# One low-part operation per weight piece, and background steps moved from the second attention to the first FFN

## The chip, the cores and the metric

The kernel runs on 1 core of one Trainium2 chip. The metric is device time in microseconds (us) of one launch. Three timed runs of the kernel before took 968.81, 970.23 and 971.09 us; the median is 970.23.

## The reference, cut

A block of 256 tokens of width 1024 passes through three layers: attention and a SwiGLU FFN twice, then a conformer convolution module and an FFN with a short convolution. Everything is fp32. Each layer has six modulation vectors, which come from one vector `c` and a 1024 x 6144 matrix; they scale, shift and gate what the layer does.

```python
c_act = silu(c)
for i in range(2):
    mod = c_act @ ada_w[i] + ada_b[i]                       # six vectors of 1024
    sh_a, sc_a, g_a, sh_f, sc_f, g_f = split(mod, 6)
    h = rms_norm(x, norm_g[i, 0]) * (1 + sc_a) + sh_a
    y = moba_attention(h, ...) if i == 0 else diff_attention(h, ...)
    x = x + g_a * rms_norm(y, norm_g[i, 1])
    h = rms_norm(x, norm_g[i, 2]) * (1 + sc_f) + sh_f
    g, u = split(h @ ffn_w_in[i], 2)                        # 1024 x 5632
    x = x + g_f * rms_norm((silu(g) * u) @ ffn_w_out[i], norm_g[i, 3])
# third layer: the same frame with its own c and matrix, a conformer module and conv_ffn
```

## The kernel before, in words

**Stages.** Six stages follow one another: first attention, first FFN, second attention (the one with two softmaxes a head), second FFN, conformer, last FFN. Between two of them stand a residual sum, a norm and transposes (`residual`, `norm_T`). In this profile the first attention runs to about 150 us, the first FFN to 338, the second attention to 473, the second FFN to 660, the conformer to 775.

**Weights.** Each weight is read once. `load` takes a raw buffer (a pool of four, 1 MiB each; a few parked tiles at the start) and issues the DMA on SP's queue. `split` then makes of each half of a raw buffer, a piece of 128 x 1024, a high part (ScalarE, line 108, a copy rounded to fp32r) and a low part (VectorE, line 110, raw minus high). Before the change the low part is two operations of 512 columns: one for each half of a row piece, or, for pieces of column blocks, one for each four of the eight row tiles. High and low parts live in `hlp`, which has eight buffers for each, so four units can be split ahead of TensorE, and the four raw buffers stand behind them. `mm3` (lines 135 to 137) makes three matmuls of each product: high x high, high x low, low x high. `cols_unit` loads 1024 rows of 256 columns, `rows_unit` 256 rows of 1024 columns, `half_unit` four row tiles of two spans.

**An FFN's loop** (`swiglu`). Eleven chunks of 256 hidden columns. Chunks 0 and 1 go first with tokens in rows. Then pass d = 0 to 10 computes the hidden columns of chunk d + 2 (`up_cols`, two column units, 96 matmuls of 256 columns; pass 7 does two chunks, the later ones none), and multiplies chunk d with `w_out` (`down_half`, one row unit, 24 matmuls of 512 columns). After `up_cols` and after the row unit of a pass `bg_step` is called: 17 calls in passes 0 to 7, two in each of 0 to 6, three in 7. The second FFN has hooks in its passes that build the conformer's stationary operands (`conv_weights`, line 463), the first has small loads and transposes (`columns`, `conv_taps`).

**An attention** projects v (four row units), then q and k of two heads at a time (eight column units). The heads' softmax chains run beside the matmuls (`block`): scores on TensorE, `sc` and `mn` on VectorE (618), exp on ScalarE (620), a transpose on TensorE (635), the product with v (641), and in the second attention a norm of each head: POOL (650, 652), `on` on VectorE (654), a transpose (657), `ol` on VectorE (659). At the end comes the output projection (four row units). `bg_step` is called after each of the 16 units of an attention.

**Background vectors.** The first two modulation vectors are made at the start. The other 16 are made by the generator `background`, one after the other, four steps a vector. A step loads 1 MiB of the matrix (`mod_load`, SP's queue, a raw buffer) and adds it to `gemv` in two VectorE operations of 1024 columns (lines 202 and 204), which are ordered behind the newest low part. The last step sums over the partitions with 8 small matmuls (232), adds the bias (235), multiplies by a gain (211 or 213), and stores the row to `scratch` with a DMA on SP's queue (214). The loads of the next bias and gain into the single tiles `bquad` and `gquad` (line 180) are on SP's queue too. `fetch`, at the end of a stage, reads the vectors that it needs and runs the steps that are missing.

**The plans.** `bg_plan(steps, slots, skip)` spreads so many steps over so many calls of `bg_step`, after `skip` calls: each call takes the steps left over the slots left, rounded up. So (16, 17) gives one step a call, and (20, 17) two in each of the first three calls and one afterwards. The line is `plans = ((12, 10, 2), (16, 17), (12, 12), (20, 17), (0, 0), (4, 4, 4))`, one entry a stage; the steps sum to 64.

**Order.** Tile's scheduler orders each engine's queue and SP's from the program order and its own model. Each queue then runs in that order.

Of the kernel before, what the change touches and what calls it, by code (L numbers as in the profile page):

```python
# [36 lines left out]
def bucket_rows():  # L37
    """One-hot rows [32, 384]: column m is the bucket of rel = 255 - m (columns past 255 are masked)."""
    exact = N_BUCKETS // 2
    rel = np.maximum(255 - np.arange(384), 0)  # L40
    nf = np.maximum(rel, 1).astype(np.float32)
    large = exact + (np.log(nf / np.float32(exact)) / np.float32(math.log(MAX_DISTANCE / exact))
                     * np.float32(N_BUCKETS - exact)).astype(np.int32)
    large = np.minimum(large, N_BUCKETS - 1)
    b = np.where(rel < exact, rel, large)
    return (b[None, :] == np.arange(N_BUCKETS)[:, None]).astype(np.float32)
# [3 lines left out]
def net(ctx: ExitStack, tc: tile.TileContext, a, out):  # L50
# [17 lines left out]

    # ---------------------------------------------------------------- weights

# [12 lines left out]
    def parked(*tags):  # L83
        """Room for the two pieces of a unit in tiles that rest between two parts of the network."""
        rooms = []
        for tag in tags:
            if tag == "q":
                for _ in range(2):
                    t = two.tile([P, 1024], F32R, name="park", tag=tag)
                    rooms.append(t)  # L90
            else:
                t = big.tile([P, 2, 1024], F32R, name="park", tag=tag)
                rooms += [t[:, 0, :], t[:, 1, :]]
        return rooms

    def split(raw, blocks=False, rooms=None):
        pieces = []
        for j in range(2):
            r = raw[:, 1024 * j:1024 * j + 1024]
            if rooms:  # L100
                h, l = rooms[2 * j], rooms[2 * j + 1]
            else:
                h = hlp.tile([P, 1024], F32R, name="h")
                l = hlp.tile([P, 1024], F32R, name="l")
            if blocks:
                r = raw.rearrange("p (k n) -> p k n", k=8)[:, :, j * P:j * P + P]
                h, l = (t.rearrange("p (k n) -> p k n", k=8) for t in (h, l))
            newest["high"] = nc.scalar.activation(h, r, AF.Copy).ins  # L108
            for k in (slice(0, 4), slice(4, 8)) if blocks else (slice(0, 512), slice(512, 1024)):
                newest["split"] = nc.vector.tensor_sub(l[:, k], r[:, k], h[:, k].bitcast(F32)).ins  # L110
            pieces.append((h, l))
        return pieces

    def rows_unit(w, k0, c0, rooms=None):
        """Two row tiles of 1024 columns; a piece is one row tile."""
        return split(load(lambda raw: [(
            raw.rearrange("p (k n) -> p k n", k=2),
            w[k0 * P:k0 * P + 256, c0:c0 + 1024].rearrange("(k p) n -> p k n", p=P))]), rooms=rooms)

    def cols_unit(w, c):  # L120
        """All eight row tiles of 256 columns; a piece is one block of 128 columns."""
        return split(load(lambda raw: [(raw.rearrange("p (k n) -> p k n", k=8),
                                        w[:, c:c + 256].rearrange("(k p) n -> p k n", p=P))]), blocks=True)

    def half_unit(w, q, cols, rooms=None):
        """Four row tiles of two 256 column spans; a piece is two row tiles of 512 columns."""
        def parts(raw):
            v = raw.rearrange("p (k n) -> p k n", k=4)
            return [(v[:, :, i * 256:i * 256 + 256],
                     w[512 * q:512 * q + 512, c:c + 256].rearrange("(k p) n -> p k n", p=P))  # L130
                    for i, c in enumerate(cols)]
        return [tuple(t.rearrange("p (k n) -> p k n", k=2) for t in hl) for hl in split(load(parts), rooms=rooms)]
# [5 lines left out]

    # -------------------------------------------------------------- constants

# [17 lines left out]

    # ------------------------------------------------------------- modulation

# [17 lines left out]
    def load_quad(vec, t, queue=nc.sync):  # L178
        """A row of 1024 as four spans of 256, on partitions 0, 32, 64 and 96."""
        queue.dma_start(t.rearrange("(g r) n -> g r n", r=32)[:, 0, :], vec.rearrange("(g n) -> g n", g=4))  # L180
        return t

    def mod_load(w, j, r, halved=False):
        """Rows 8 p + 2 r and 8 p + 2 r + 1 of a vector's 1024 columns."""
        src = w[:, j * D:j * D + D].rearrange("(p k) n -> p k n", k=8)[:, 2 * r:2 * r + 2, :]
# [4 lines left out]
    def mod_sum(w, j, c):  # L190
        """Per-partition partial sums of c @ w[:, vector j]; yields after each quarter, the tile last."""
        t = None
# [24 lines left out]
    def quads(ps, c, k, src, start, stop):  # L217
        """ps[32 q:32 q + 32] += c[k] * the span q of 256 of the row, summed over the partitions."""
        for q in range(4):
# [4 lines left out]
    def mod_vector(w, b, j, g, slot, c):  # L224
        """Vector j of a layer's modulation, into the scratch; yields after each quarter of the rows."""
        bq = load_quad(b[j * D:j * D + D], bquad)
# [12 lines left out]

    # vector j of a layer: shift, scale, gate of the mixer, then of the ffn  # L240
    jobs = []
# [42 lines left out]
    def first_norm(T):  # L284
        """The first layer's scale and shift, turned into columns, and what they make of x: only the shift's part
        waits for all of their weights."""
        bias = [bquad, gquad]
# [56 lines left out]

    # ------------------------------------------------------------ small inputs

    nb = big.tile([P, NH, S], F32, name="nb")

    def bias_tiles():
        """nb[p, h, k] = -bias of head h for query - key = 127 + p - k, masked where negative: the rows of the  # L350
        Toeplitz matrix start one further left on each partition, which is a step back, so they are read
        upside down and flipped by the permutation."""
        st = hlp.tile([P, 1024], F32, name="stage", tag="h")
# [77 lines left out]
    def conv_taps():  # L431
        """taps[32 j + c, m, 4 t + g] = tap 4 m + j of channel 128 t + 32 g + c."""
        w = a["a_dw_w_2"][0]
# [16 lines left out]
    def conv_weights(ts):  # L450
        """Stationary operands of the depthwise convolution: four taps of 32 channels stacked on the rows."""
        for t in ts:
# [15 lines left out]

    # ------------------------------------------------------------------ norms

# [4 lines left out]
    def rstd_of(ss):  # L475
        """(the sum of the two columns + eps)^-0.5."""
        v = small.tile([P, 1], F32, name="var")
# [5 lines left out]
    def scaled(src, by, tag="hn"):  # L483
        """The two halves of a row times a vector, and what normalises the row."""
        ss = small.tile([P, 2], F32, name="ss")
# [44 lines left out]
    def project(T, w, c0, tags=(), between=None, early=0, before=None):  # L530
        """[256 tokens, 1024] = T @ w[:, c0:c0+1024]; yields the two banks of each half of the tokens."""
        ps = [[acc.tile([P, 512], F32, name="acc") for _ in range(2)] for _ in range(2)]
# [19 lines left out]
    def cols_matmul(ps, T, unit, between=None):  # L552
        """ps[:, b, :] = features of block b, all 256 tokens."""
        for b, (wh, wl) in enumerate(unit):
# [5 lines left out]
    def lead(T, w, cols, count):  # L560
        """As cols_matmul for the first 2 * count blocks of both column spans, with tokens in rows until turned;
        the first half of the tokens is done before the second is asked for."""
        units, tiles = [], []
# [36 lines left out]

    # -------------------------------------------------------------- attention

    def block(diff, h, blk, q, kk, v, T):
        """One head, 128 queries: their attention over the keys up to them, into T[:, h, block]."""
        nk = P * (blk + 1)
# [109 lines left out]

    # -------------------------------------------------------------------- ffn

# [85 lines left out]

    # -------------------------------------------------------------- conformer

# [172 lines left out]

    # ---------------------------------------------------------------- network

# [13 lines left out]
    stages.append((2, 5, lambda T: conv_ffn(T, a["f_up_w_2"][0], a["f_down_w_2"][0])))  # L994
    plans = ((12, 10, 2), (16, 17), (12, 12), (20, 17), (0, 0), (4, 4, 4))

# [41 lines left out]
```

## Time and profile before

| | |
|---|---|
| timed runs | 968.81, 970.23, 971.09 us |
| span of the profiled execution | 967.0 us |
| TensorE busy | 928.9 us (96%) |
| VectorE busy | 767.5 us (79%) |
| ScalarE busy | 495.1 us (51%) |
| low parts, line 110, 512 columns, `l` and parked tiles | 548 and 24 operations of 0.68 us |
| background, lines 202 and 204 | 16 and 112 operations |
| DMA | 244 MB, mean 252 GB/s |

The span goes from the first to the last instruction of the profiled execution, whose own device time isn't given apart from the three runs; their median is 3.2 us longer than this span. Matmuls are pipelined, so a busy TensorE isn't one at its peak: its rows of busy time hide short waits, and starts of matmuls show them. A line number is that of the kernel; the changed kernel's lines after 109 are one less.

### The profile page before, as it was taken

How to read it: one execution, taken by the hardware profiler on the slowest of the kernel's cores; microseconds unless marked ns; L12 is line 12 of the kernel's file. 1: busy time of each engine (PE TensorE's matmuls, PEld its weight loads, DVE VectorE, ACT ScalarE, POOL GpSimd, SP SyncE). 2: the span in 40 equal slices, each digit the busy share in tenths (PEclk: the TensorE clock that was granted, in tenths of full speed). 3: DMA queues.
4: the chain of work that ended last, by engine and by line, in shares of the span. 5: the costliest groups of instructions: out<-in, count | busy, mean ns of one | idle time of the engine just before them, and what ended most of it. 6: DMA issues, size and time to landing. Idle time of an engine off the chain costs nothing.

```text
span 967.0 us, 17220 instructions
## 1 busy us (share of the span) xinstructions
PE 928.9 (96%) x6687; PEld 811.4 (84%) x6687; DVE 767.5 (79%) x1461; ACT 495.1 (51%) x870; POOL 51.2 (5%) x118
## 2 busy tenths in 40 slices
PE   5899999999999999999999999999999899999997
PEld 2579977998999879876799989987897779999996
DVE  1779977976878798887999878888777789977774
ACT  2355665543344445675634444555416755655552
POOL 2100000000000010122100000001000100000000
PEclk9999999999999999999999999999999999999999
DMA  9988885978879859673588899786747466975511
GB/s 349 390 318 293 316 283 176 322 283 317 282 272 382 300 185 348 225 259 106 167 285 320 311 345 336 275 303 204 269 113 201 142 208 226 302 231 188 175 45 44
DMA packets 141519, 244.06 MB, mean 252 GB/s; under 512 B 6662, under 2 KB 106174, under 8 KB 141438
## 3 DMA queue, kind: packets, MB, share of 16 engines
q1 hardware_dynamic: 140918, 241.64, 72.1%
q0 software_dynamic: 496, 1.31, 0.4%
q8 instruction: 52, 0.85, 0.4%
q14 instruction: 29, 0.24, 0.1%
q10 hardware_dynamic: 24, 0.01, 0.0%
HBM read 240.94 MB, written 2.01 MB: 251 GB/s over the span
## 4 chain that ended last, share of the span: by engine, by line
issue 44%; PE 30%; DVE 4%; POOL 4%; ACT 2%; DMA 1%; SPq 0%; DVEq 0%; POOLq 0%; ACTq 0%
PE up L137 5%; PE up L136 5%; PE up L135 5%; PE acc L135 4%; PE acc L137 4%; PE acc L136 4%; PE acc L851 1%; DVE l L110 1%; POOL rstd L480 1%; POOL var L478 1%; ACT h L108 1%; POOL orstd L652 1%; ACT junk L473 1%; POOL ovar L650 1%; DMA raw<-in_f_up_w_dram 1%
## 5 line engine op out<-in xcount | busy, mean ns | idle before, releaser
L110 DVE TENSOR_TENSOR l<-raw,h 128x512 fp32r<-128x512 f32 x548 | 354.7, 684 | 80.6 <-ACT h L108 78.2
L108 ACT ACTIVATE h<-raw 128x1024 fp32r<-128x1024 f32 x274 | 280.1, 1053 | 171.1 <-PE up L136 38.0
L137 PE MATMUL up<-th,l 128*128 128x256 f32 x640 | 181.7, 284 | 0.0
L136 PE MATMUL up<-tl,h 128*128 128x256 f32 x640 | 181.1, 283 | 0.0
L135 PE MATMUL up<-th,h 128*128 128x256 f32 x640 | 180.8, 282 | 0.0
L204 DVE SCALAR_TENSOR_TENSOR gemv<-raw,c_s,gemv 128x1024 f32<-128x1024 f32 x112 | 143.2, 1279 | 0.9
L135 PEld LDWEIGHTS up<-th,h 128*128 128x128 f32 x640 | 121.0, 189 | 2.0 <-DVE ml L747 0.4
L137 PEld LDWEIGHTS up<-th,l 128*128 128x128 f32 x640 | 120.7, 189 | 0.1
L136 PEld LDWEIGHTS up<-tl,h 128*128 128x128 f32 x640 | 120.4, 188 | 0.4
L135 PE MATMUL acc<-h,mh 128*128 128x512 f32 x232 | 91.6, 395 | 0.1
L136 PE MATMUL acc<-l,mh 128*128 128x512 f32 x232 | 90.9, 392 | 0.0
L137 PE MATMUL acc<-h,ml 128*128 128x512 f32 x232 | 90.5, 393 | 0.0
L137 PE MATMUL up<-oh,l 128*128 128x256 f32 x288 | 81.9, 284 | 0.0
L136 PE MATMUL up<-ol,h 128*128 128x256 f32 x288 | 81.7, 284 | 0.0
L135 PE MATMUL up<-oh,h 128*128 128x256 f32 x288 | 81.1, 282 | 0.0
L135 PE MATMUL acc<-th,h 128*128 128x256 f32 x256 | 75.1, 293 | 0.1
L137 PE MATMUL acc<-th,l 128*128 128x256 f32 x256 | 73.8, 288 | 0.2 <-DVE l L110 0.2
L136 PE MATMUL acc<-tl,h 128*128 128x256 f32 x256 | 72.7, 284 | 0.0
L135 PEld LDWEIGHTS up<-oh,h 128*128 128x128 f32 x288 | 54.6, 189 | 0.8
L136 PEld LDWEIGHTS up<-ol,h 128*128 128x128 f32 x288 | 54.2, 188 | 0.7
L137 PEld LDWEIGHTS up<-oh,l 128*128 128x128 f32 x288 | 54.4, 189 | 0.1
L135 PEld LDWEIGHTS acc<-h,mh 128*128 128x128 f32 x232 | 43.6, 188 | 11.1 <-issue 2.5
(230 smaller groups left out, 1663.7 us busy)
## 6 DMA issues: line engine op xcount, KB each, us to landing
raw<-in_ada_w_dram SPq DMA_DIRECT2D x46, 1024.0 KB
raw<-in_ffn_w_in_dram SPq DMA_DIRECT2D x36, 1024.0 KB
raw<-in_mod_w_dram SPq DMA_DIRECT2D x24, 1024.0 KB
raw<-in_ffn_w_out_dram SPq DMA_DIRECT2D x22, 1024.0 KB
raw<-in_f_up_w_dram SPq DMA_DIRECT2D x18, 1024.0 KB
raw<-in_moba_w_qkv_dram SPq DMA_DIRECT2D x12, 1024.0 KB
raw<-in_diff_w_qkv_dram SPq DMA_DIRECT2D x12, 1024.0 KB
raw<-in_f_down_w_dram SPq DMA_DIRECT2D x11, 1024.0 KB
```

Of the source, the lines that this page charges most:

```text
L108: newest["high"] = nc.scalar.activation(h, r, AF.Copy).ins
L110: newest["split"] = nc.vector.tensor_sub(l[:, k], r[:, k], h[:, k].bitcast(F32)).ins
L135: nc.tensor.matmul(ps, lh, rh, start=start, stop=False, skip_group_check=True)
L136: nc.tensor.matmul(ps, lh, rl, start=False, stop=False, skip_group_check=True)
L137: nc.tensor.matmul(ps, ll, rh, start=False, stop=stop, skip_group_check=True)
L204: nc.vector.scalar_tensor_tensor(t, src, c[:, k:k + 1], t, op0=ALU.mult, op1=ALU.add)
L473: nc.scalar.activation(junk, src, AF.Square, scale=1.0 / 32, accum_out=ss[:, i:i + 1])
L478: nc.gpsimd.tensor_scalar(v, ss[:, 0:1], ss[:, 1:2], EPS, op0=ALU.add, op1=ALU.add)
L480: nc.gpsimd.tensor_tensor(r, v, mhalf, op=ALU.pow)
L650: nc.gpsimd.tensor_scalar(var, ss, 1.0 / DH, EPS, op0=ALU.mult, op1=ALU.add)
L652: nc.gpsimd.tensor_tensor(rn, var, mhalf, op=ALU.pow)
L851: mm = nc.tensor.matmul(ps[32 * g:32 * g + 32, 0:P], lw[t][:, m, g, :], ur[:, g, 4 * m:4 * m + P], start=m == 0, stop=m == 7, tile_positio ...
```

## The change

Two edits. `split` makes the low part of a piece in one operation of 1024 columns. The plans of the first three stages become (15, 10, 2), (25, 17) and (5, 12). All else of the diff is docstrings and comments turned into blank lines.

```diff
             newest["high"] = nc.scalar.activation(h, r, AF.Copy).ins
-            for k in (slice(0, 4), slice(4, 8)) if blocks else (slice(0, 512), slice(512, 1024)):
-                newest["split"] = nc.vector.tensor_sub(l[:, k], r[:, k], h[:, k].bitcast(F32)).ins
+            newest["split"] = nc.vector.tensor_sub(l, r, h.bitcast(F32)).ins
             pieces.append((h, l))
...
-    plans = ((12, 10, 2), (16, 17), (12, 12), (20, 17), (0, 0), (4, 4, 4))
+    plans = ((15, 10, 2), (25, 17), (5, 12), (20, 17), (0, 0), (4, 4, 4))
```

## Rows read from the trace of the kernel before

**Rows 1.** The page's first part: busy us, share of the span, instructions

```profile
span 967.0 us, 17220 instructions
...
PE 928.9 (96%) x6687; PEld 811.4 (84%) x6687; DVE 767.5 (79%) x1461; ACT 495.1 (51%) x870; POOL 51.2 (5%) x118
```

**Rows 2.** Stretches: us, busy PE, PEld, DVE, ACT, POOL, clock, DMA share, GB/s

```profile
25.00:50.00 25.00, 20.99 (x125) 14.96 (x118) 18.32 (x35) 11.20 (x16) 2.70 (x4) 0.93 1.02 392
...
60.00:80.00 20.00, 19.66 (x155) 18.46 (x153) 15.33 (x30) 11.51 (x17) 0.00 (x0) 1.00 1.00 351
80.00:90.00 10.00, 10.00 (x84) 9.16 (x83) 9.23 (x23) 5.00 (x14) 0.00 (x0) 1.00 0.70 247
172.80:190.00 17.20, 17.20 (x125) 16.21 (x124) 16.54 (x26) 8.56 (x13) 0.00 (x0) 1.00 1.01 351
...
172.80:244.20 71.40, 71.40 (x508) 65.05 (x507) 56.10 (x92) 31.04 (x42) 0.00 (x0) 1.00 0.88 311
...
493.30:511.20 17.90, 17.90 (x134) 16.27 (x132) 16.16 (x26) 6.24 (x11) 0.00 (x0) 1.00 0.97 353
```

**Rows 3.** Groups by line and shape: busy us, mean ns of one, idle before

```profile
L110 DVE TENSOR_TENSOR l<-raw,h 128x512 fp32r<-128x512 f32 x548 | 354.7, 684 | 80.6 <-ACT h L108 78.2
...
L204 DVE SCALAR_TENSOR_TENSOR gemv<-raw,c_s,gemv 128x1024 f32<-128x1024 f32 x112 | 143.2, 1279 | 0.9
...
L498 DVE SCALAR_TENSOR_TENSOR x<-hn,rstd,x 128x512 f32<-128x512 f32 x24 | 17.0, 749 | 4.6 <-POOL rstd L480 4.5
...
L463 DVE TENSOR_TENSOR dwl<-taps,sel 128x128 f32<-128x128 f32 x48 | 10.7, 284 | 0.0
L232 PE MATMUL tr<-gemv,ones 128*32 128x256 f32 x128 | 10.2, 391 | 0.0
```

**Rows 4.** VectorE in order of time, both FFNs: start us, us, operation

```profile
166.51 1.29 DVE L110 TENSOR_TENSOR l<-raw,h 128x512 fp32r<-128x512 f32 x2 [3.83 <-ACT h L108]
...
181.35 2.49 DVE L110 TENSOR_TENSOR l<-raw,h 128x512 fp32r<-128x512 f32 x4
...
488.15 1.30 DVE L110 TENSOR_TENSOR l<-raw,h 128x512 fp32r<-128x512 f32 x2
...
508.50 1.29 DVE L110 TENSOR_TENSOR l<-raw,h 128x512 fp32r<-128x512 f32 x2 [1.49 <-ACT h L108]
...
529.15 1.90 DVE L110 TENSOR_TENSOR l<-raw,h 128x512 fp32r<-128x512 f32 x3 [0.72 <-ACT h L108]
```

**Rows 5.** TensorE in order of time, at the first matmuls of FFN passes

```profile
172.80 0.36 PE L135 MATMUL up<-th,h 128*128 128x256 f32 x1
190.05 0.28 PE L135 MATMUL up<-th,h 128*128 128x256 f32 x1
...
190.28 0.28 PE L137 MATMUL up<-th,l 128*128 128x256 f32 x1
...
493.35 0.37 PE L135 MATMUL up<-th,h 128*128 128x256 f32 x1
...
511.15 0.39 PE L135 MATMUL up<-th,h 128*128 128x256 f32 x1
...
528.13 0.28 PE L135 MATMUL up<-th,h 128*128 128x256 f32 x1
```

**Rows 6.** What SP's queue waited for, 475 to 560 us: us, times, longest

```profile
SPq L214 <- DVE row L211: 7.1, 1, 7.1
```

**Rows 7.** First attention: TensorE and ScalarE in order of time, waits in brackets

```profile
67.79 0.39 PE L137 MATMUL acc<-th,l 128*128 128x256 f32 x1 [0.23 <-DVE l L110]
...
65.95 2.00 ACT L108 ACTIVATE h<-raw 128x1024 fp32r<-128x1024 f32 x2 [2.35 <-DMA raw<-in_moba_w_qkv_dram]
```

**Rows 8.** Who waited for whom, 378 to 468 us: us, times, longest

```profile
PE tr L635 <- DVE ol L659: 1.7, 3, 0.8
PE tr L657 <- DVE on L654: 0.9, 1, 0.9
...
PEld tr L635 <- DVE ol L659: 3.3, 5, 1.2
```

## The prediction

> **What bounds the kernel now.** The page comes first: TensorE is busy for 928.9 us, 96% of the span [rows 1], so a change elsewhere counts only where it makes TensorE wait or lets it stop waiting. Where it waits is not seen in shares of the span. So I read next the stretches of single stages [rows 2]: in the first FFN (some 150 to 338 us) and the second (473 to 660) TensorE is busy in every microsecond, and the DMA share is near 1.0 at the start of each. Then the costs of single operations [rows 3], and then the quantity on which this case turns: how long before TensorE takes a split weight its split was ready. I call it the lead. For one loop pass of an FFN I count VectorE's low-part operations in program order, take the end of the one that completes the first block of both units of the pass [rows 4], and subtract it from the start of that pass's first matmul [rows 5]. TensorE takes the second unit's block only 24 matmuls of 0.12 us (190.05 to 190.28 us are two [rows 5]), 2.9 us, after that start, so it stands still only when the lead falls under -2.9 us.
>
> First FFN: 172.80 - 167.80 = 5.0 us in pass 0, 190.05 - 182.63 = 7.4 in pass 1. Second FFN: 493.35 - 488.83 = 4.5, 511.15 - 509.79 = 1.4, 528.13 - 530.43 = -2.3 in passes 0, 1, 2. The first FFN gives one background step to each of its slots, two in a pass. The second gives four in its pass 0, three in pass 1 and two afterwards. So the trace already holds a price for doubled slots: the second FFN lost 3.1 us of lead in its pass of four steps and 3.7 in the pass of three, and came within 0.6 us of stopping TensorE.
>
> **The change, part by part.** *The split.* 572 low-part operations of 512 columns become 286 of 1024. In a run they start 0.60 us apart (four in 2.49 us [rows 4], one lasts 0.68 [rows 3]), so a pair takes 1.20. The new one: L204 with 1024 columns lasts 1.279, L498 with 512 of the same kind 0.749 [rows 3], so 512 columns are 0.53 us and the new operation lasts 0.68 + 0.53 = 1.21, with the next start some 1.13 after its own. It saves between 0 and 0.07 us, at most 20 us of VectorE in all, and none of it is on TensorE's path while the lead is positive. Against it: what needs the first half alone gets it 0.53 us later. That counts where TensorE already waits for a half, as it does in the first attention (0.23 us for L110 at 67.79) [rows 7]; such shifts don't add up, since the next unit comes at its own time. I take +0.3, ends -0.5 and +2.
>
> *The steps.* A step is one 1 MiB load on SP's queue into one of the four raw buffers and two VectorE operations. Four steps make a vector, which adds 8 small matmuls (10.2 / 16 = 0.64 us of TensorE [rows 3]), one or two operations of 256 columns, loads of bquad and gquad, and a store of the row to scratch, all on SP's queue. The plans before sum to 64 steps, which are all there are (16 vectors). The plans after sum to 69, so the second FFN gets 19 of its 20 and the last stage none. Finished vectors by stage go from 3, 4, 3, 5, 0, 1 to 3, 7, 1, 5, 0, 0: TensorE's 0.64 us only change place between stages in which it is the bound, cost 0.
>
> *First attention, 12 to 15 steps in 10 slots.* The slots 3 to 5 take two instead of one, behind the first three column units. There the DMA share is 1.00 at 351 GB/s [rows 2] and ScalarE waits 2.35 us for a weight load [rows 7], so there is hardly any lead. A load at that rate is 1.049 / 0.351 = 3.0 us, three are 9.0 if all show. Less shows if they fill holes: the DMA share falls to 0.70 in 80 to 90 us [rows 2]. I take +2, ends 0 and 9.
>
> *First FFN, 16 to 25 steps in 17 slots.* The first 8 slots take two: four steps in each of passes 0 to 3. A pass then loads 3 + 4 = 7 units, 7.34 MB, instead of 5. The four passes last 71.4 us (172.8 to 244.2) [rows 2] and would want 29.4 MB, 411 GB/s. The trace shows 351 GB/s at a share of 1.01 in pass 0 of this FFN and 353 at 0.97 in pass 0 of the second [rows 2]. VectorE: 56.10 us busy in the four passes [rows 2], plus 8 steps of two operations (20 us by L204's row), less 24 pieces x 0.07, is 74 of 71.4. Both are short. The nearest row is the second FFN's pass of four steps: -3.1 us of lead a pass, four times -12.4; some of the 3.1 belongs to L463, of which 32 operations of 0.28 us [rows 3] fell into the second FFN alone. The cover is 5.0 + 2.9 = 7.9 us, so TensorE stands for 4.5 us. What could hide all of it: 29.4 MB at the 392 GB/s of 25 to 50 us [rows 2] takes 75.0 us, 3.6 too many, within the cover. What could make it worse: SP's queue is in order, and the store of a finished row stands in it until the row is there, once for 7.1 us with the next loads behind it [rows 6]. A vector would end in each of these passes, not in every second. If such holds cost each pass 3 us more, 16 us in all. I take +4.5, ends 0 and 16.
>
> The Trainium skill, page "DMA: Bandwidth & Descriptors", section Specifications, gives one core's share of the memory as about 358 GB/s. The 392 of the trace stands above it. By the page 29.4 MB would be 82 us, 10.7 too many and 2.8 us of standstill (an estimate from that page); by the 392 there is none.
>
> *Second attention, 12 to 5 steps.* The five go one each to the first five slots, four of them in the v projection. The heads' loop loses 7 steps, some 17 us of VectorE, and after its first unit has none. What TensorE waits for in this stage is the heads' small operations, which stand in VectorE's queue between splits and steps: 1.7 us for L659 and 0.9 for L654 on TensorE itself, 3.3 on its weight loads for L659 [rows 8]. The gain is between 0 and 3.3; below nothing only by the coarser splits, 0.5. I take -2.5.
>
> *Second FFN.* Its passes keep their steps (4, 3, 2, ...; only the last is missing), and its splits get shorter: 0, since the lead never reached -2.9. *Last stage.* 4 loads fewer beside its start: -0.3, ends -1 and 0. ScalarE's and POOL's queues get nothing.
>
> **The sum.** 0.3 + 2 + 4.5 - 2.5 - 0.3 = +4.0. The profiled execution has a span of 967.0 us [rows 1]; the three timed runs have a median of 970.23, so 3.2 us lie around the span and stay. 970.2 + 4.0 = 974.2 us, slower.
>
> **The rivals.** *Even.* The four passes run at the rate of 25 to 50 us, the lead falls but TensorE doesn't stop, and the attention terms cancel: 970.23 + 0.3 + 2 - 2.5 - 0.3 = 969.7. For it: in the new mix four of seven loads are of that kind of rows. Against it: the second FFN's pass of four steps made 353, and there too four of seven were. Chance 0.18. *Faster.* The heads' chain in the second attention is the one place where the steps cost TensorE time now. If VectorE is free there, L659 and L654 come when needed, in the stretch of 400 to 460 us: -3.3, with -1 in the last stage, and nothing lost in the first attention: 970.23 - 4.3 = 965.9. It decides as soon as the first FFN's lead stays over -2.9. For it: rows 8 name those two. Against it: the first FFN's bill. Chance 0.26. *The plan isn't what runs.* Tile's scheduler orders each queue by its own model, and it could put the added loads later, where there is room; then nothing but the splits shows: 970.5. Against it: in the second FFN the doubled slots are seen where the plan has them. Chance 0.04.
>
> **How the numbers follow.** The forecast, loads run short in the first FFN, has 0.52. Below 0.2% (1.94 us, about what a measurement of this kernel can tell from no change) count the even case and the unused plan, 0.22. So slower 0.52, same 0.22, faster 0.26. The low end must take in most of the faster case, 965.5. The high end: 4.5 becomes 12 in the first FFN, three quarters of the way to its bound, and the rest stays, 981.7; with some of the first attention's bound 983.5.
>
> **What would show it.** Right: a DVE group at L109 of 286 operations near 1.2 us; in the first FFN a lead that falls by about 3 us a pass to pass 4, matmuls of L134 to L136 with idle time before them for a low part or a high part between 220 and 260 us, a DMA share near 1.0 there; 5 steps in the second attention and less waiting on L658. Wrong: a first FFN as long as before (17.85 us a pass) with lead left over; a first attention longer by much more than 2 us; a new operation longer than 1.3 us; waits in the heads' chain that stay although the steps are gone.

## The result: 4.0% slower, most of it in the first FFN

The changed kernel takes 1008.26 us (median of four runs, 1006.44 to 1010.45); the kernel before, run beside it, 969.52. The ratio is 1.0399, with an interval of 1.0379 to 1.0419. The sign is the forecast's, the size is not: 38.7 us instead of 4.0, above the range. The profiled execution went from 967.0 [rows 1] to 1008.7 us.

The page's first part of the changed kernel:

```profile
span 1008.7 us, 16917 instructions
...
PE 944.9 (94%) x6687; PEld 823.0 (82%) x6687; DVE 757.3 (75%) x1175; ACT 494.9 (49%) x870; POOL 53.6 (5%) x118
```

TensorE is busy for 16 us more with the same 6687 instructions, and stands idle for 26 us more. VectorE is busy for 10 us less. So two things have to be explained: why TensorE waited, and why the same matmuls took longer.

I cut the execution at first matmuls that both kernels have, and subtract. The stretches of before begin at 59.0 us (first attention, q and k), 118.4 (its output projection), 172.8 (first FFN, pass 0), 319.7 (pass 7's first matmul with `w_out`; behind it stand the FFN's end and the v projection), 368.9 (second attention, q and k), 432.1 (its output projection), 468.5 (second FFN). The change makes them longer by:

| stretch | forecast | measured |
|---|---|---|
| first attention, q and k with heads | +2 (0 to 9) | +10.4 |
| first FFN, pass 0 to pass 7 | +4.5 (0 to 16) | +28.4 |
| first FFN's end and v projection | not in the sum | +4.7 |
| second attention, q and k with heads | -2.5 for both | +1.2 |
| second attention, output projection | | -1.6 |
| all the rest | -0.3, and the split's +0.3 anywhere | -1.4 |

The stretches in the view by windows (us, busy PE, PEld, DVE, ACT, POOL, clock, DMA share, GB/s); of before, those that [rows 2] doesn't hold:

```profile
59.00:118.40 59.40, 59.06 (x471) 54.99 (x469) 52.10 (x116) 36.07 (x74) 0.00 (x0) 1.00 0.90 320
172.80:319.70 146.90, 146.90 (x1079) 136.39 (x1077) 116.01 (x187) 65.56 (x89) 0.00 (x0) 1.00 0.89 315
```

and of the changed kernel:

```profile
60.10:129.80 69.70, 61.59 (x472) 56.90 (x471) 58.20 (x103) 36.05 (x73) 0.00 (x0) 0.98 0.88 317
183.30:358.60 175.30, 160.71 (x1095) 146.67 (x1094) 130.15 (x153) 59.18 (x83) 0.00 (x0) 0.93 0.80 288
```

The first FFN's 28.4 us are 14.6 of idle TensorE (175.3 - 160.7) and 13.8 of longer business. The granted clock of 0.93 shows the second part. It sits in four stretches at half the clock, 1.2 instead of 2.4 GHz, of the changed kernel:

```profile
222.20:229.00 6.80, 6.17 (x27) 5.88 (x28) 5.60 (x6) 3.38 (x4) 0.00 (x0) 0.50 0.76 274
249.60:256.40 6.80, 6.11 (x28) 6.11 (x29) 4.51 (x5) 2.00 (x2) 0.00 (x0) 0.50 1.04 396
276.90:280.20 3.30, 3.30 (x18) 3.30 (x17) 3.30 (x4) 1.30 (x2) 0.00 (x0) 0.50 0.01 4
314.50:321.20 6.70, 6.52 (x29) 6.22 (x30) 6.65 (x6) 2.82 (x3) 0.00 (x0) 0.50 1.00 382
```

They sum to 23.6 us. The FFN has 16 more small matmuls than before, 1.3 us by their rows; 12.5 of the 13.8 remain. The Trainium skill, page "TensorE: Matmul & The Clock Gate", section Terms, puts the penalty at throttled time times the share of pulses gated; by it these stretches cost 11.8 us (an estimate from that page), and the trace agrees with its 12.5.

And the DMA share is lower than before, 0.80 against 0.89. That speaks against the forecast's mechanism, a shortage of load rate, as the whole cause. What the waits say of the engines in the first FFN, 183 to 340 us (us, times, longest):

```profile
ACT h L108 <- DMA raw<-in_ffn_w_in_dram: 13.8, 7, 4.0
...
DVE gemv L201 <- PE tr L231: 9.3, 5, 3.9
...
PE up L134 <- ACT h L108: 6.4, 4, 3.5
```

and of SP's queue, 183 to 375 us:

```profile
SPq L80 <- DVE gemv L203: 35.7, 14, 7.9
SPq L213 <- DVE row L212: 15.9, 3, 8.9
...
SPq L415 <- PE tr L409: 6.7, 1, 6.7
```

A wait of SP's queue for a raw buffer, as in the first of these rows, is no loss by itself: the kernel before has 19.7 us of the same kind in ten (150 to 340 us). The wait of L201 is new in this stage. A background vector is summed in the one tile `gemv`; the next vector's first operation (L201) overwrites it, so VectorE waits until TensorE's eight small matmuls (L231) have read the last one. One such wait in order of time (start us, us), first VectorE,

```profile
228.66 2.61 DVE L203 SCALAR_TENSOR_TENSOR gemv<-raw,c_s,gemv 128x1024 f32<-128x1024 f32 x2 [0.83 <-DMA raw<-in_ada_w_dram]
...
238.19 0.76 DVE L201 TENSOR_SCALAR gemv<-raw,c_s 128x1024 f32<-128x1024 f32 x1 [2.16 <-PE tr L231]
...
240.68 1.21 DVE L109 TENSOR_TENSOR l<-raw,h 128x1024 fp32r<-128x1024 f32 x1
```

then TensorE,

```profile
237.48 0.64 PE L231 MATMUL tr<-gemv,ones 128*32 128x256 f32 x8
```

and SP's queue:

```profile
227.86 3.80 SPq L80 DMA_DIRECT2D raw<-in_ada_w_dram  x2
238.33 2.53 SPq L415 DMA_DIRECT2D rowsf<-in_f_dw_w_dram  x2
240.97 0.88 SPq L80 DMA_DIRECT2D raw<-in_ffn_w_in_dram  x1
```

The vector is summed at 231.3. TensorE comes to its eight matmuls only at 237.5, because they stand in its queue behind matmuls of the FFN. VectorE's queue is in order: it stands idle for 2.16 us before L201, and the split at 240.68 is among what comes behind that. SP's queue stands as well, but in this place for another reason: from 231.7 to 238.3, the 6.7 us of its third row, it waits to issue a small load into `rowsf`, one of the small loads of `columns`, until TensorE has made a transpose (L409) that stands right behind the eight matmuls. The FFN's next weight is issued behind it, at 240.97. What TensorE waits for is then issued late because TensorE is late. That is a theory read off the trace. The runs below test the part of it that comes from the one `gemv` and from a vector's end; none takes the hold at `rowsf` away, which the kernel before has too (4.1 us at the longest).

In the second attention the rows that answer to [rows 8] are (420 to 512 us):

```profile
PEld tr L634 <- DVE ol L658: 1.5, 2, 0.9
...
PE tr L634 <- DVE ol L658: 0.9, 2, 0.7
PE tr L656 <- DVE on L653: 0.8, 1, 0.8
```

The waits named in the forecast did get shorter, 5.9 to 3.2 us, but the stage as a whole did not.

The new operation is as forecast, 1.22 us (group by line: busy us, mean ns, idle before):

```profile
L109 DVE TENSOR_TENSOR l<-raw,h 128x1024 fp32r<-128x1024 f32 x274 | 328.8, 1220 | 92.4 <-ACT h L108 88.4
```

### The profile page after: what moved, and what is told of

It reads as the page before. It is cut to its first block, busy times and chain, and to the rows that moved or that the text cites. A ratio compares the mean times of both kernels' runs of the same rounds, so it can differ in the third digit from the quotient of the medians.

```text
span 1008.7 us, 16917 instructions
## 1 busy us (share of the span) xinstructions
PE 944.9 (94%) x6687; PEld 823.0 (82%) x6687; DVE 757.3 (75%) x1175; ACT 494.9 (49%) x870; POOL 53.6 (5%) x118
## 4 chain that ended last, share of the span: by engine, by line
issue 44%; PE 39%; DMA 5%; ACT 4%; POOL 3%; DVE 3%; SPq 1%; POOLq 0%; DVEq 0%; ACTq 0%
PE acc L136 6%; PE acc L134 6%; PE acc L135 6%; PE up L136 5%; PE up L135 5%; PE up L134 5%; ACT h L108 2%; DMA raw<-in_moba_w_qkv_dram 2%; POOL var L477 1%; ACT junk L472 1%; DMA x<-in_x_dram 1%; PE acc L850 1%; POOL rstd L479 1%; PE up L614 1%; PE up L640 1%
## 5 line engine op out<-in xcount | busy, mean ns | idle before, releaser
L109 DVE TENSOR_TENSOR l<-raw,h 128x1024 fp32r<-128x1024 f32 x274 | 328.8, 1220 | 92.4 <-ACT h L108 88.4
L134 PE MATMUL up<-th,h 128*128 128x256 f32 x640 | 186.1, 291 | 6.6 <-ACT h L108 6.4
L136 PE MATMUL up<-th,l 128*128 128x256 f32 x640 | 184.6, 290 | 3.1 <-DVE l L109 3.1
L135 PE MATMUL up<-tl,h 128*128 128x256 f32 x640 | 185.1, 289 | 0.0
L134 PEld LDWEIGHTS up<-th,h 128*128 128x128 f32 x640 | 125.8, 196 | 10.6 <-ACT h L108 8.7
L136 PEld LDWEIGHTS up<-th,l 128*128 128x128 f32 x640 | 124.8, 196 | 3.5 <-DVE l L109 3.5
L135 PEld LDWEIGHTS up<-tl,h 128*128 128x128 f32 x640 | 125.3, 196 | 0.2
L738 ACT ACTIVATE sg<-up 128x256 f32<-128x256 f32 x44 | 16.8, 381 | 117.0 <-PE up L136 71.8
L477 POOL TENSOR_SCALAR var<-ss 128x1 f32<-128x1 f32 x24 | 15.3, 637 | 763.2 <-ACT junk L472 582.5
```

Of the source, the lines that this page charges most:

```text
L109: newest["split"] = nc.vector.tensor_sub(l, r, h.bitcast(F32)).ins
L134: nc.tensor.matmul(ps, lh, rh, start=start, stop=False, skip_group_check=True)
L135: nc.tensor.matmul(ps, lh, rl, start=False, stop=False, skip_group_check=True)
L136: nc.tensor.matmul(ps, ll, rh, start=False, stop=stop, skip_group_check=True)
L477: nc.gpsimd.tensor_scalar(v, ss[:, 0:1], ss[:, 1:2], EPS, op0=ALU.add, op1=ALU.add)
L738: nc.scalar.activation(g, ps[:, 0:256], AF.Silu)
```

## The experiments

Theories: *bandwidth* (the forecast's: loads come too slowly), *vector's end* (VectorE and SP's queue stand on the end of one vector and the start of the next), *VectorE* (its added operations are what is short), *rooms* (background loads hold the four raw buffers). Each run's loss against before by the stretches of the table above, in us, from the one profiled execution of each; the ratio is that of the timed runs. The two don't always agree: the profiled execution of e10 is the longest of three, 3.9 us above their median, that of e11 the shortest of six, 4.1 us below. So a difference of 2 or 3 us between two rows of this table says little.

| run | ratio | 1st attention | FFN passes | FFN's end, v | 2nd heads | 2nd output |
|---|---|---|---|---|---|---|
| the change | 1.0399 | +10.4 | +28.4 | +4.7 | +1.2 | -1.6 |
| e1 split only | 1.0055 | -0.9 | +0.1 | +0.1 | -0.8 | +6.4 |
| e2 plans only | 1.0402 | +7.8 | +25.2 | +5.2 | +1.7 | -1.0 |
| e3 first attention's plan | 1.0163 | +10.6 | +0.7 | +0.2 | -2.0 | +6.1 |
| e4 phase | 1.0305 | +17.3 | +15.1 | +4.6 | -0.3 | -1.6 |
| e6 two gemv | 1.0308 | +12.1 | +16.2 | +2.3 | +2.3 | -1.4 |
| e7 narrow | 1.0376 | +10.0 | +24.3 | +2.5 | -0.3 | -1.6 |
| e8 no loads | 0.9993 | +2.1 | +2.2 | +1.1 | -1.2 | -1.6 |
| e9 small loads | 1.0161 | -1.0 | +19.6 | +1.1 | -1.3 | -1.7 |
| e10 gemv, side queue | 1.0228 | +9.1 | +14.2 | +4.3 | -0.3 | -1.6 |
| e11 the same, small loads | 1.0063 | +0.7 | +3.4 | +1.5 | -1.1 | -1.6 |

**Which edit.** e1 is the change with before's plans, e2 the kernel before with the new plans.

```diff
-    plans = ((15, 10, 2), (25, 17), (5, 12), (20, 17), (0, 0), (4, 4, 4))
+    plans = ((12, 10, 2), (16, 17), (12, 12), (20, 17), (0, 0), (4, 4, 4))
```

> The split's low part is one operation of 1024 columns, and the plan of background steps is that of before. Bandwidth theory (the forecast's: the added steps are short of load rate in the first FFN) and room theory (a background load keeps one of the four raw buffers until VectorE's in-order queue comes to it, and the loads of the pass wait behind it) both expect the split to do next to nothing alone: 969.5 + 0.3, between 969.0 and 971.5. Rival, the coarse split is what hurts: the first half of a unit comes 0.53 us later everywhere, and the first attention and the first FFN already lose with the old plan: 980 or more. Rival, the split helps by itself: the 20 us of VectorE show, 967 or less.

> The plan of the changed kernel with the halved split of before. Bandwidth and room theories: all of the loss is the plan's, 1008 +- 2. If the coarse split and the plan only hurt together (a half that comes late meets a step), well under 1000. If the shorter VectorE work was a relief that the plan needs, more than 1010.

e1 took 975.47 us, 1.0055 (1.0042 to 1.0068): by the ratio 5.3 us, more than the forecast's end of 2 and than the 971.5 that both theories allowed. e2 took 1009.32, 1.0402 (1.0386 to 1.0418). So the plans make the whole loss, and the split's 5.3 do not add to it. e1's 6.4 us lie in one place, between the second attention's output projection and the second FFN. On TensorE, of e1:

```profile
472.85 1.97 PE L511 MATMUL tr<-ident,hn 128*128 128x128 f32 x8 [4.19 <-DVE hn L507]
```

and on ScalarE:

```profile
465.11 2.95 ACT L108 ACTIVATE h<-raw 128x1024 fp32r<-128x1024 f32 x3
```

TensorE has run out of matmuls and waits 4.19 us for the next stage's norm (the waits for it in before are 0.41 us at the longest); before it, that norm's squares stood on ScalarE behind three high parts in a row. The order of the queues is another one: the last transposed head stands behind 77 of the 96 matmuls of the output projection, in before behind 64, in the changed kernel behind 61. So fewer matmuls are left to cover the norm. e3 below, in the same order (77), loses 6.1 there.

e3 keeps the split and gives 15 steps to the first attention alone.

```diff
-    plans = ((15, 10, 2), (25, 17), (5, 12), (20, 17), (0, 0), (4, 4, 4))
+    plans = ((15, 10, 2), (13, 17), (12, 12), (20, 17), (0, 0), (4, 4, 4))
```

> The new split, 15 steps in the first attention, then 13, 12 and 20 as before's plan would have gone on: one step in a slot of the first FFN. The trace of the changed kernel puts the first attention 10.4 us longer and the first FFN 28. If the two losses are separate, this kernel is 969.8 + 10.4 = 980, and its first FFN lasts as long as before's, passes of about 18 us. If the first FFN's loss is a consequence of the three added steps of the first attention (no lead is carried over), it shows here too: 1000 or more. If the first attention's loss is taken back later, 972.

986.57 us, 1.0163 (1.0150 to 1.0177), more than the 980 expected by the 6.1 us that e1 loses too. The losses are separate: the first attention's 10.6 stay, and the FFN with one step in a slot runs as before.

**The vector's end.** In the changed kernel 15 steps are done when the first FFN starts, so the last step of a vector and the first of the next (16 and 17, 20 and 21, ...) are the two steps of one slot. e4 shifts this by one.

```diff
-    plans = ((15, 10, 2), (25, 17), (5, 12), (20, 17), (0, 0), (4, 4, 4))
+    plans = ((16, 10, 2), (24, 17), (5, 12), (20, 17), (0, 0), (4, 4, 4))
```

> As the changed kernel, but 16 and 24 steps instead of 15 and 25: the same loads in the first FFN less one, still two in each of its first seven slots, yet a vector now ends with a slot and the next begins with a slot, where in the changed kernel the end of one vector and the start of the next stand in the same slot. Vector-boundary theory (VectorE's first operation of the next vector waits 9 us for the eight small matmuls of the last one, which stand in TensorE's queue behind the FFN's): the first FFN loses 5 us or so instead of 28, with 3 us more in the first attention, 988 in all. Bandwidth theory and room theory without the boundary: the first FFN loses as much as in the changed kernel, 1008 to 1011.

1000.36 us, 1.0305 (1.0289 to 1.0320). The FFN's loss falls from 28.4 to 15.1, and VectorE's wait from 9.3 us in five to (190 to 340 us):

```profile
DVE gemv L201 <- PE tr L231: 2.5, 2, 1.4
```

The FFN's 15.1 are not the 5 or so, nor the whole the 988, that the theory of the vector's end gave; something is left. The fourth added step of the first attention cost 6.9 us in this execution, more than each of the three before it. e4 has also one doubled slot less in the FFN, so e6 mends the cause itself: every second vector is summed in a buffer of the pool `coef`.

```diff
+                    at["n"] += 1
-                    t = one.tile([P, D], F32, name="gemv")
+                    t = coef.tile([P, D], F32, name="coef") if at["n"] % 2 else one.tile([P, D], F32, name="gemv")
```

> The changed kernel, every second background vector summed in a buffer of the pool coef, so that the next vector's first operation doesn't wait until TensorE has read the last vector. Boundary theory (the one buffer gemv makes VectorE, and behind it the splits of the pass, wait for eight small matmuls in TensorE's queue, 9.3 us five times): the first FFN falls from +28 us to +10 or less and the whole to about 990. Rooms theory (the raw buffers that background loads hold): 1005 or more. Bandwidth theory: unchanged, 1008.

999.85 us, 1.0308 (1.0288 to 1.0329). The wait is gone from the list and the FFN loses 16.2: between these two executions the one buffer made 12.2 of 28.4, and by the ratios 8.8 us of the whole kernel. But 16.2 is more than the 10 that the theory allowed for; something else holds too. The FFN's window of e6:

```profile
184.50:347.60 163.10, 155.29 (x1094) 142.22 (x1093) 129.92 (x153) 59.64 (x83) 0.00 (x0) 0.96 0.87 310
```

**VectorE, loads, bytes.** e7 takes VectorE's work away and leaves loads and queues, e8 takes the loads away and leaves the work, e9 leaves both but an eighth of the bytes.

```diff
 e7: nc.vector.scalar_tensor_tensor(t[:, 0:64], src[:, 0:64], c[:, k:k + 1], t[:, 0:64], ...)
 e8: src = flat          # a constant tile, no mod_load
 e9: raw = load(lambda raw: [(raw[:, 0:256], src8)]);  src = raw[:, 0:256] four times
```

> The changed kernel with every background operation of VectorE on 64 of 1024 columns (the modulation vectors are not what they should be); loads, rooms, matmuls and queues stay. If VectorE's added 1.2 us operations are what is short (20 us in the first FFN's first four passes, and behind them the splits), the first FFN comes down to within 8 us of before and the first attention's +10 to +5 or less: 975 or less. If bytes or rooms are short: the first FFN keeps at least 15 of its 28 us, and the total is 990 or more.

> The changed kernel without the loads of the background vectors after the first two (63 MB less in all; VectorE's operations read a constant tile, so the modulation vectors are not what they should be). Operations, matmuls, row stores and small loads stay. If bytes or the raw buffers that these loads hold are the cause, the loss goes with them: first attention and first FFN as in before, 970 or less, even below (TensorE's waits for loads in the first attention go too). If VectorE's operations and the vector boundary are the cause: the first FFN keeps 15 us or more, the total is 990 or more.

> The changed kernel with each background load cut to an eighth of its bytes (128 KB into 256 of the 2048 columns, from which VectorE's operations, of full length, read; the modulation vectors are not what they should be). Each still takes one of the four raw buffers until VectorE has come to it. Bandwidth theory: as without the loads, 975 or less. Rooms and boundary theory: the first FFN keeps most of its 28 us, 995 or more, though its DMA share falls by a quarter.

The FFN's windows of e7,

```profile
185.60:356.80 171.20, 157.89 (x1095) 142.96 (x1093) 85.86 (x151) 59.60 (x83) 0.00 (x0) 0.95 0.82 295
```

of e8,

```profile
173.50:322.60 149.10, 149.10 (x1094) 137.37 (x1093) 135.71 (x160) 65.92 (x89) 0.00 (x0) 1.00 0.60 199
```

and of e9, its first attention ahead of its FFN:

```profile
61.60:120.00 58.40, 57.43 (x469) 54.31 (x467) 56.29 (x101) 37.02 (x74) 0.00 (x0) 1.00 0.74 244
...
174.70:341.20 166.50, 156.31 (x1094) 143.47 (x1092) 135.50 (x159) 65.85 (x90) 0.00 (x0) 0.95 0.61 204
```

e7 took 1006.49 us, 1.0376 (1.0356 to 1.0397): VectorE falls from 130 to 86 us, and the FFN still loses 24.3. VectorE's work is not what is short. e8 took 969.23, 0.9993 (0.9982 to 1.0003): without the loads nearly all is gone, though VectorE does as much as ever. VectorE's wait for the small matmuls is still there (2.5 us in three, with one `gemv`), and TensorE is never idle in this FFN: the vector's end costs time only together with the loads. e9 took 986.05, 1.0161 (1.0130 to 1.0192): in the first attention the loss is gone, so there it was bytes; in the FFN 19.6 of 28.4 stay at a DMA share of 0.61, so there bytes are the smaller part.

**What is left.** e10 is e6 with the loads of `bquad` and `gquad` and the store of the row on POOL's queue, so that SP's queue doesn't stand on a vector's end; e11 is e10 with e9's small loads.

```diff
-        nc.sync.dma_start(scratch[slot].rearrange("(g n) -> g n", g=4),
+        nc.gpsimd.dma_start(scratch[slot].rearrange("(g n) -> g n", g=4),
...
-        bq = load_quad(b[j * D:j * D + D], bquad)
+        bq = load_quad(b[j * D:j * D + D], bquad, nc.gpsimd)
```

> The changed kernel with the second buffer for gemv (a run before: first FFN +16 us instead of +28) and with the background's loads of bquad and gquad and the store of its row on POOL's queue, so that nothing of a vector's end stands in SP's queue ahead of weight loads. If SP's queue standing on a vector's end is the rest: the first FFN at most +8, the step into the second attention at most +1, and the total 985 to 990 (the first attention keeps its +10). If the rest is bytes or raw buffers: the first FFN stays at +14 or more, the total at 997 to 1000.

> As the kernel with both mends, and each background load cut to an eighth of its bytes (the modulation vectors are not what they should be). What is left in the first FFN is then neither bytes, nor the vector's end, but the raw buffers that a background load holds until VectorE has used it. If the bytes are the rest: first attention and first FFN as in before, 970 +- 2. If the raw buffers are: the first FFN stays 8 us or more too long, 980 or more.

e10 took 991.39 us, 1.0228 (1.0205 to 1.0251), e11 976.67, 1.0063 (1.0049 to 1.0076). Both lie between the times that the expectations gave to their two theories, so neither is the whole rest. By the ratios the side queue is worth 7.8 us of the whole kernel (e6 to e10); of that the FFN's rows show 2.0 (16.2 to 14.2), but e10's profiled execution is one of its long ones, so the FFN's share stays open. The bytes are the larger part of what is left: 14.2 to 3.4 in the FFN when they go. The two parts nearly add: the mends take 14.2 us from the FFN with full loads and 16.2 with small ones (e9 to e11), the smaller loads 8.8 without the mends and 10.8 with them. What is left in e11's profile is 3.4, of which 1.3 are small matmuls; more than that the raw buffers alone don't cost in that execution, which is 4.1 us shorter than e11's median.

e10's FFN, then its passes 1, 2 and 3:

```profile
183.40:344.50 161.10, 155.05 (x1094) 141.00 (x1092) 131.22 (x155) 61.33 (x85) 9.60 (x16) 0.97 0.90 319
...
201.40:219.20 17.80, 17.80 (x129) 16.24 (x129) 15.63 (x18) 7.64 (x11) 1.76 (x3) 1.00 1.04 386
219.20:238.80 19.60, 19.30 (x134) 16.57 (x132) 14.91 (x22) 4.43 (x8) 2.22 (x3) 1.00 0.70 246
238.80:262.30 23.50, 20.19 (x131) 17.79 (x130) 18.65 (x23) 7.72 (x13) 1.13 (x2) 0.92 1.02 371
```

and of its SP queue, 160 to 345 us:

```profile
SPq L418 <- PE tr L412: 8.1, 1, 8.1
```

With the vector's holds gone the DMA share stands at 1.0 in passes 1 and 3: here is the shortage that the forecast spoke of, and which the changed kernel's trace hides, since its queues don't even ask for the bytes. Passes 0 and 1 last 18.0 and 17.8 us on the lead that was there, as forecast. But it isn't the rate alone that then makes pass 3 last 23.5. In pass 2, which is doubled too, the share is 0.70: SP's queue stands for 8.1 us, up to 231.7, at the small load into `rowsf`. At pass 1's 386 GB/s pass 2 would have moved 2.7 MB more, 7 us of loads (an estimate from these two rows). How much of the rest is this hold and how much the rate no run tells. TensorE is idle for 6.1 us in this FFN; the other 8.1 are its lower clock and the small matmuls.

**Is there a gain anywhere?** b1 is the kernel before with e10's two mends; b2 moves also four steps, (20, 17) and (8, 12); c3 moves the four steps without the mends.

> The kernel before, its split and its plan, with the two mends (second buffer for gemv, the vector's end on POOL's queue). The kernel without any background loads took 0.9993 of before, so there is hardly anything to win from where these loads stand: 968.5 to 970.5, the same. If the vector's end costs the attentions something even with one step in a slot (SP's queue stood 7.1 us on a row there): 966 or less.

> As the kernel before with the two mends, and four steps moved from the second attention to the first FFN (20 and 8 instead of 16 and 12): two steps in each of its first three slots, with vectors that end with a slot. If two steps in a slot are harmless once the vector's end holds nobody: the first FFN as before, and the second attention's last part 1 to 1.6 us shorter, 967 to 969. If the loads' bytes or buffers cost TensorE time in any case (some 2 us for each doubled slot): 973 or more.

> The kernel before with nothing but four steps moved from the second attention to the first FFN (20 and 8). The forecast's gain of the second attention is 7 steps for 2.5 us, so 4 steps for 1.4: 968.5. If steps there cost nothing (the kernel without any background loads took 0.9993 of before): 969.5 to 971. If three doubled slots cost the first FFN something: 972 or more.

b1: 973.04 us, 1.0022 (1.0011 to 1.0033). b2: 971.50, 1.0015 (1.0006 to 1.0024). c3: 977.92, 1.0082 (1.0069 to 1.0095). No version beats before, which fits e8. b1 is slower than either of its expectations, b2 lies between its two: with one step in a slot the mends win nothing and cost 2.1 us by the ratio, where isn't known. In c3 the FFN's passes lose 0.4 us, so three doubled slots are free there, with vectors that end with a slot; but the stretch with the FFN's end and the v projection loses 6.1, in b2 1.1. A first suspect is SP's queue, here of c3,

```profile
328.83 0.53 SPq L214 DMA_DIRECT2D scratch<-row  x1
329.40 0.44 SPq L169 DMA_DIRECT2D coef<-scratch  x1
329.88 0.43 SPq L80 DMA_DIRECT2D raw<-in_diff_w_qkv_dram  x1
```

and of b2:

```profile
314.30 0.39 SPq L80 DMA_DIRECT2D raw<-in_diff_w_qkv_dram  x1
```

A vector ends with the FFN in c3, its row is ready only at 328.8, and the second attention's weights are issued behind the store, 8.2 us into the stretch. The changed kernel does the same: its store is issued at 365.98 and its first v weight at 367.04, 8.4 us into the stretch. Before issued that weight at 306.90, 12.8 us ahead of it. In b2 the store is on POOL's queue, and the weight 6.5 us ahead. But the late weight isn't enough: e6 and e7 issue theirs 8.5 us into the stretch, and lose 2.3 and 2.5; e10, with the store on POOL's queue, issues it 1.9 us ahead and loses 4.3. What TensorE waits for in this stretch of c3 is not a weight but a norm:

```profile
PE tr L512 <- DVE hn L508: 4.6, 2, 3.0
```

In b2 these waits are 2.3 us, in before 2.1. And the windows of the stretch, of c3 and then of b2, differ in the clock:

```profile
321.60:376.90 55.30, 50.74 (x227) 39.95 (x226) 43.59 (x65) 24.84 (x40) 3.50 (x8) 0.94 0.73 264
```

```profile
320.80:371.10 50.30, 47.90 (x226) 37.67 (x225) 38.44 (x57) 22.25 (x37) 7.05 (x13) 1.00 0.66 241
```

So the stretch is lost by a longer wait for the norm and the lower clock around it (0.97 in the changed kernel, 1.00 in e6 and e7). What makes that wait longer, the late store among others, isn't settled.

**The split again.** c1 is e1 with the split in halves in the second attention alone; c2 is the new split with 20 and 8 steps.

```diff
+            for k in half if at_stage["i"] == 2 else (whole,):
+                newest["split"] = nc.vector.tensor_sub(l[:, k], r[:, k], h[:, k].bitcast(F32)).ins
```

> The new split and the old plan, but the split in halves in the second attention alone. If the split's 5.3 us are lost by what stands beside it in the last part of that stage (the second half of the last heads' chain comes later in TensorE's order, and the norm behind it has 4.2 us without cover): 970 +- 1.5, and the stage from the o-projection to the second FFN as long as in before. If the coarser operation costs a little everywhere: 973 or more.

> The new split with 20 steps in the first FFN and 8 in the second attention. If the split's loss needs the steps that stand in the heads' loop beside it (with 5 steps there it isn't seen): 970 +- 2. If it is the split's alone: 974 to 976, as with the old plan.

c1: 974.11 us, 1.0048 (1.0036 to 1.0061). c2: 975.11, 1.0060 (1.0047 to 1.0073). In c1's trace the loss at the output projection falls from 6.4 to 1.6, as expected of the place, but the ratio is hardly lower: the output projection isn't all of it, and the rest of the loss lies in parts of 1 to 2.5 us (the first stretch, the second attention's heads, the last stages), as the theory of a coarser operation that costs a little everywhere expected. In c2 the place loses nothing (-1.6), and its 4.5 lie in the FFN's end and v projection, where c3 with halves loses 6.1. So the price of the coarse split is +5.3 with before's plan (e1), nothing with the new one (the change against e2), and -2.1 by the ratios with the plan of c2 and c3. It is not a property of the operation; it goes with the order of the queues. Which difference of order costs how much isn't settled.

## Why the prediction was wrong, and where it was right

**The first FFN, the step that failed most.** The sum took the second FFN's pass of four steps as the nearest row for a pass with two doubled slots, -3.1 us of lead. It is the same number of steps at another phase: 40 steps were done before that FFN, so vectors ended with a slot, and 15 before this one, so they ended inside one. The runs showed 28.4 us in place of 4.5: 15.1 when only the phase is shifted, with one doubled slot less (e4), 16.2 with a second `gemv` (e6), 14.2 with the vector's end on another queue too (e10), 3.4 with small loads besides (e11). The prediction didn't ask which tiles of a step are single and who reads them. A sign of it stood in the list of groups of before, with the wait for the small matmuls behind the second bar:

```profile
L202 DVE TENSOR_SCALAR gemv<-raw,c_s 128x1024 f32<-128x1024 f32 x16 | 12.0, 748 | 2.5 <-PE tr L232 2.3
```

The prediction spoke of `bquad` and `gquad` and named SP's queue as the place of a hold (its upper bound of 16). One hold was on VectorE's queue, 12.2 us in the profiles and 8.8 by the timed runs (e6); SP's was real as well, 7.8 us of the whole kernel by the timed runs (e10), so the bound of 16 had a cause but only one of several.

**The named mechanism was there, but the nearness of its number is luck.** Freed of the vector's holds, the FFN shows the DMA at 1.0 and two passes of cover, and 6.1 us of idle TensorE (e10) where 4.5 were forecast. But those 6.1 come behind 8.1 us in which SP's queue stood at `rowsf`, which the forecast didn't have, and the price of a pass came from the wrong row. And the time is 14.2, not 6.1: every estimate took an idle microsecond as one, while in these rows the clock fell to half behind the waits. In the changed kernel 14.6 us of idle cost 28.4. VectorE as the second shortage, "74 of 71.4", was wrong: e7 takes a third of its work away and 24.3 us stay. (The high end's 12 is called three quarters of the way to its bound; it is three quarters of the bound of 16.)

**The first attention.** +2 was taken between 0 and 9, because holes in the DMA share seemed free; the measured 10.4 is above that upper end. The stretch moved 320 x 59.4 = 19.0 MB before and 317 x 69.7 = 22.1 MB after: three loads more at the same rate, and the share of 0.90 became 0.88, so no hole was filled. Three loads are 9.0 us, and the clock of 0.98 in 69.7 us is about the other 1.4. With small loads the loss is gone (e9, e11). Doubled slots with no lead cost their full loads.

**The second attention.** -2.5 was taken from waits that did get shorter (-1.6 at the output projection, and -1.0 to -1.7 in every run with fewer steps there). Against it the stretch ahead of it lost 4.7, and the heads 1.2, which the sum didn't have. The 4.7 are longer waits for the norm and a lower clock; their cause stays open, and so does that of the 1.2. The prediction counted what the moved steps free in this stage, and put at nothing what happens where a vector's end, a norm and SP's queue meet between two stages.

**The split.** The operation measured 1.22 us where 1.21 was worked out. Its effect on the time, +0.3 with an end of +2, was wrong as a term of its own (+5.3 alone); that it came out near nothing in the change as a whole (e2) is luck of the order of the queues.

**Second FFN and last stage.** -0.8 and -0.7 us, near the 0 and -0.3 of the sum. The matmuls of the vectors that moved into the first FFN, taken at zero as they only change place, show as 1.3 us there. The plan did run where it was written, against that rival; the even case and the faster one fell with the first FFN.

## What to carry to other kernels

Before moving hidden work, run a kernel without it: here 969.23 against 969.9 us (e8) said that there was next to nothing to win. It is no strict bound, since e8 is the changed kernel, and the order of the queues alone moved 5 us (e1). When a step is doubled, ask for each tile of it whether it is single and in which in-order queue its reader stands, and where in the slots its end falls; a row from another phase is no price for it. And an idle microsecond of TensorE can cost more than one: 28.4 us for 14.6 idle in this FFN, 10.4 for 7.8 more in the first attention.

## What the runs showed of the hardware

The granted clock fell to 0.50 behind short waits. TensorE of the changed kernel, in order of time:

```profile
222.68 0.58 PE L134 MATMUL up<-th,h 128*128 128x256 f32 x1 [3.47 <-ACT h L108]
...
314.53 0.58 PE L134 MATMUL up<-th,h 128*128 128x256 f32 x1 [2.08 <-ACT h L108]
```

The stretches at half speed that hold these two starts lasted 6.8 and 6.7 us. Of the FFNs above, only those without idle time, before's and e8's, and e11's with 0.8 us of it, show a clock of 1.00 throughout.

One core moved 386 GB/s for 17.8 us in e10's pass 1. The Trainium skill, page "HBM Reference", section Specifications (TRN2), says that a core that streams alone measures well above its share of about 358; the trace agrees. The forecast's estimate by a page went by the share.
